# Hybrid decoder block on one core: plain pairs for differential attention and the first gates, GpSimd transfers in written order, normalising chunk by chunk, plain pairs emptied block by block

## The chip, the cores and the metric

One core of one Trainium2 chip runs the whole program. Its engines are PE (TensorE, matmul; PEld is its weight load), DVE (VectorE), ACT (ScalarE), POOL (GpSimd) and SP (SyncE), which here only issues transfers. The metric is the device time of one execution in microseconds, the median of three runs. A profile is one further execution, so sums are made against that execution's own time.

## What is computed

One decoder layer of width 2048 over 256 tokens, in float32:

```python
h = rmsnorm(x, norm_mix)
proj = h @ w_in                     # dq dk dv | conv in | rq rk rv rg | 3 x 2048 gates
ya = diff_attention(rope(dq), rope(dk), dv, lam)    # softmax(map 0) - lam * softmax(map 1)
yb = silu(layernorm(conv(ca * sigmoid(cb))))        # 31 taps, causal
yr = silu(rg) * groupnorm(retention(rope(rq), rope(rk), rv))
merged = sum(sigmoid(gates[i]) * (y @ w_branch[i])) # i = 0 ya, 1 yb, 2 yr
x = x + merged @ w_out
x = x + cross_attention(rmsnorm(x), rmsnorm(mem))   # wq, wkv, wo; 4 heads, 256 memory tokens
x = x + swiglu(rmsnorm(x))                          # w13: 2 x 5632 columns, w2
return rmsnorm(x, norm_final)
```

All weights are read from HBM once; the activations of the layer stay on the chip but for a few spills.

## The kernel before, in words

**One product.** A weight matrix is cut into column blocks of 512 and depth chunks of 512. A half chunk (256 deep, 128x1024 elements in the chip's layout) is loaded by SP into a tile `raw` (10 buffers), and is then split in two parts: ACT casts it to `wh` (high part, type fp32r) and DVE subtracts to get `wl` (the rest). The activations are held in the same two parts (`hi`, `lo` of an `Act`). A product is three matmuls of 128x512: high by high, high by rest, rest by high. A half chunk against both token halves is one *unit* of 12 matmuls. The parts are made up to LA = 4 units ahead of their matmuls.

**Plain and S pairs.** Column blocks go in pairs. In a plain pair (`win` with MODES0, function `block`) the two blocks run one after the other, each chunk costs 4 units, 48 matmuls for both blocks, and `evac` reads the PSUM tile `mm` (2 buffers) straight away. In an S pair (function `pair`) some chunks, marked S in MODES1 = "SNNN" and MODES2 = "SSNN", are done by a scheme with 7 products of block matrices in place of 8 (`quad_jobs`): 7 units of 6 matmuls, so 42. For these DVE adds raw tiles (2 per chunk), two GpSimd transfers add a quarter of the weights onto a raw tile (`f2`, line 367, whose sum is used by unit p7, and `f6`, line 383, whose sum is used by p4), 7 casts and 7 subtractions make the parts, four PSUM tiles `tp` take intermediate sums, and `join1`, `join5`, `join6`, `join7` (1 ACT copy and 5 DVE operations of 128x512) and two `done` (one DVE addition of 128x1024 each) put the result together before `evac` reads it from SBUF. The S chunks need factors of the activations (`factors`: 4 small DVE operations, a cast and a subtraction), kept in `shi` and `slo`.

**The first pair of a stage.** `pair_n` runs the first pair on activations that are not yet scaled by the row norm: for each of the four chunks first both halves of block 0, then both of block 1, and `after(c)` behind chunk c; `evac0` and `evac1` follow at the end. `normalise` meanwhile makes scaled copies (`xn` from `xa`; `x2n` from `x2T`) for the pairs that follow: at `after(1)` it waits for the norm, starts `spread` (which broadcasts it) and four tasks `chunk(c)`; each adds the parts, multiplies, splits again, and makes factors for the chunks in `sc`.

**Order of work.** All is emitted as a list of units and calls. Side work (rope, conv, attention, normalising) is written as Python generators; `pump` advances each by one step after every unit, `drain` and `need` run one to its end where its result is wanted. A list scheduler with a simulated clock then sets the order on each engine. SP's loads are held to the written order by `tc.keep_in_program_order` (`ld`); the DMAs that GpSimd issues are not.

**Stages.** In order: conv inputs (pair_n on blocks 8 and 6, then 9 and 7), retention of 2 groups (4 plain pairs), differential attention (`diff_qk(0)`, `win(4, 5, ...)`, `diff_qk(1)`, all MODES1), three times gates (2 S pairs, MODES2, each followed by two branch blocks), memory keys and values (4 S pairs on `w_kv`), `w_out` (2 S pairs), queries and cross attention, `w_o` (2 plain blocks and an S pair), SwiGLU (pair_n, then 10 S pairs on `w_13`, and between them twice 2 S pairs on `w_2` with `x2` reloaded by `load_x2`), and the last blocks of `w_2` with the final norm, for which `load_gf` and `load_x2` fetch six tiles.

Nearly every instruction is recorded under line 85, the wrapper that issues it, so groups are told apart by the tiles that they write and read. Line 93 is SP's load.

Of the kernel before, what the change touches and what calls it, by code (L numbers as in the profile page):

```python
# [44 lines left out]
class Act:  # L45


    def __init__(self):
        self.hi = None
        self.lo = None  # L50
        self.shi = None
        self.slo = None
        self.task = None


@with_exitstack
def trunk(ctx, tc, xT, xtok, memT, memtok, w_in, w_br, w_out, w_q, w_kv, w_o, w_13, w_2,
          prm, cst, decay, gfin, out):
    nc = tc.nc
# [29 lines left out]
    sc = Pinned(nc.scalar, "act" in PIN)  # L89
    ve = Pinned(nc.vector, "dve" in PIN)  # L90
    pe = Pinned(nc.tensor, "pe" in PIN)
    def ld(**kw):
        tc.keep_in_program_order(nc.sync.dma_start(**kw))

# [20 lines left out]
    active = []  # L115
    said = {}
    wants = {}
    cap = [4]

    def spawn(gen, want=1):  # L120
# [19 lines left out]
                step(g)  # L140

    def drain(g):
        if g in active:
            settle(cap[0] - wants[g], g)
            while step(g):
                pass
# [178 lines left out]
    def quad_jobs(pp, ps0, ps1, w0, w1, a):  # L325

        def unit(ps, key, k0, t, kind, fn, **w):
            def add():  # L330
                load(**w)
                u = add_unit([(ps, key, k0, t, kind)], a)
                u["alloc"] = alloc_tp1 if ps is pp else alloc_mm
                groups.append(([u], lambda: fn(u)))
                return u
            return add

        def alloc_tp1(ps, key):
            ps[key] = TP()

        b21, b22 = w0[:, 2:4, :], w1[:, 2:4, :]
        ix = {}

        def load(**k):
            for n, w in k.items():
                ix[n] = add_chunk(w)

        def add(o, x):
            ve.tensor_tensor(out=o, in0=o, in1=x, op=ALU.add)

        def parts(u, src):
            parts_of(u)
            hi_of(u, src)
            lo_of(u, src)

        t = {}

        def f1(u):
            t["a"] = raw(ix["b11"])
            parts(u, t["a"])  # L360
            raws.pop(ix["b11"])

        def f2(u):
            r = raw(ix["b21"])
            t["b"] = raw(ix["b12"])
            add(t["a"], t["b"])
            nc.gpsimd.dma_start(out=t["b"], in_=b22, accum_op=ALU.add)  # L367
            parts(u, r)
            raws.pop(ix["b21"])
            raws.pop(ix["b12"])  # L370

        def f5(u):
            parts(u, t["a"])

        def f3(u):
            r = raw(ix["b22"])
            add(t["a"], r)
            parts(u, r)
            raws.pop(ix["b22"])

        def f6(u):
            parts(u, t["a"])
            nc.gpsimd.dma_start(out=t["a"], in_=b21, accum_op=ALU.add)  # L383

        def f7(u):
            parts(u, t.pop("b"))

        def f4(u):
            parts(u, t.pop("a"))

        return dict(p1=unit(pp, 1, 0, 0, "n", f1, b11=w0[:, 0:2, :]),
                    p2=unit(ps0, 0, 2, 0, "n", f2, b21=b21, b12=w1[:, 0:2, :]), p5=unit(pp, 5, 0, 0, "s", f5),
                    p3=unit(ps1, 0, 0, 3, "s", f3, b22=b22), p6=unit(pp, 6, 0, 1, "s", f6),
                    p7=unit(pp, 7, 0, 2, "s", f7), p4=unit(ps0, 1, 2, 1, "n", f4))

# [78 lines left out]
    def pair_n(W0, W1, acts, evac0, evac1, after):  # L474

        ps0, ps1 = {}, {}
        us = []
        for c in range(len(acts)):
            us += half_jobs(ps0, [W0[c]], [acts[c]])
            us += half_jobs(ps1, [W1[c]], [acts[c]])  # L480
            call(lambda c=c: after(c))
        call(lambda: evac0(ps0["m"]))
        call(lambda: evac1(ps1["m"]))
        close(us)


    prm_t = cpool.tile([P, PCOLS], F32, name="prm_t")
# [29 lines left out]
    def load_actT(a, src, g, c):  # L517

        def gen():
            r = S4([P, 4, 256])  # L520
            nc.gpsimd.dma_start(out=r, in_=src[c])
            yield
            for k in range(0, 4, 2):
                actT_part(a, r, g, c, (k, k + 1))
                yield
        return gen()
# [99 lines left out]
        sc.copy(a.hi, q)  # L626
        ve.tensor_tensor(out=a.lo, in0=q, in1=a.hi.bitcast(F32), op=ALU.subtract)

    def normalise(src, dst, rs, sc=SC):

        st = {}
        freed = []

        def chunk(c):
            while len(freed) <= c:
                yield
            drain(st["task"])
            q = whole(src[c])
# [9 lines left out]

        def after(c):
            freed.append(c)  # L650
            if c == 1:
                rs()
                st["task"] = spawn(spread(st, rs.tile))
                for i in range(4):
                    dst[i].task = spawn(chunk(i))
        return after

    class Rstd:
# [202 lines left out]
    def win(n0, n1, modes, evac0, evac1):  # L861
# [3 lines left out]
        else:  # L865
# [1 line left out]
            block(w_in, n1, xn, evac1)  # L867

    pair_n([w_in[8, c] for c in range(4)], [w_in[6, c] for c in range(4)], xa, ev_cb(0, rsx), ev_ca(0, rsx),
           normalise(xa, xn, Rstd(rsx, lambda: drain(st_task)), (0,)))  # L870
    win(9, 7, MODES0, ev_cb(1), ev_ca(1))


# [32 lines left out]
    def ret_group(g):  # L906
        st = {}

        def ev_v(ps):
            st["v"] = act(ps, AF.Identity, None)  # L910
            d = S4([P, 4, 256])
            nc.gpsimd.dma_start(out=d, in_=decay[g])
            st["d"] = d

        def ev_g(ps):
# [59 lines left out]

    def ev_dv(g):
        def f(ps):
            dst2[g]["v"] = ps
            ya[g].task = spawn(diff_task(g, dst2[g]), 2)
        return f  # L980

    def diff_qk(g):
        win(0 + g, 2 + g, MODES1, ev_rope(dst2[g], "q", 32, 0), ev_rope(dst2[g], "k", 32, 0))

    def diff_task(g, st):
        drain(st["qt"])
# [76 lines left out]
    for g in range(2):  # L1063
        ret_group(g)
    diff_qk(0)
    win(4, 5, MODES1, ev_dv(0), lambda ps: dst2[1].update(v=ps))
    diff_qk(1)
    call(lambda: setattr(ya[1], "task", spawn(diff_task(1, dst2[1]), 2)))

# [37 lines left out]
            a.task = spawn(add_factors(a))  # L1107
        return f

    call(later(xn[1]))  # L1110
    for bi, (br, ys) in enumerate(((2, yr), (1, yb), (0, ya))):
        if bi == 1:
            call(split_yb)
        for nb in (0, 2):
            if bi == 2 and nb == 2:
                call(lambda: mtask.append(spawn(mem_stats())))
            win(18 + 4 * br + nb, 19 + 4 * br + nb, MODES2, ev_gate(nb), ev_gate(nb + 1))
            if bi == 2 and nb == 2:
                call(lambda: mem_chunks())
            for n in (nb, nb + 1):  # L1120
# [8 lines left out]
    mst = {}  # L1129

    def mem_stats():
        yield from tok_stats(memtok, rsm, nc.gpsimd.dma_start)
        yield from spread(mst, rsm)

    def mem_chunk(c):
        r = S4([P, 4, 256])
        nc.gpsimd.dma_start(out=r, in_=memT[c])
        drain(mtask[0])
        yield
        times(r, mst["rb"])  # L1140
# [11 lines left out]

    def ev_kv(dst):
        def f(x):
            nc.gpsimd.dma_start(out=dst, in_=x)
        return f

    def mT_factors():
# [13 lines left out]
    def residual(W, acts, xin, aT, gname, rs, parts, spill=None):  # L1172
# [3 lines left out]
        def ev(nb):  # L1176
            def f(ps):
# [2 lines left out]
                xs[nb] = r  # L1180
                if spill is not None:
                    xs[nb] = None
                    nc.gpsimd.dma_start(out=spill[nb], in_=r)

                def gen():
                    sumsq(r, parts[:, nb, :])
# [20 lines left out]
    def reload_x(nbs):  # L1207
        for nb in nbs:
            xre[nb] = S4([P, 2, 512])
            nc.gpsimd.dma_start(out=xre[nb], in_=xtok[nb])  # L1210

    x1T = [Act() for _ in range(4)]
    rs1 = cpool.tile([P, 2], F32, name="rs1")
# [25 lines left out]
    def prep_kv(h):  # L1239

        def gen():
            k, v = S4([P, 2, 512]), S4([P, 2, 512])
            nc.gpsimd.dma_start(out=k, in_=kM[h])
            nc.gpsimd.dma_start(out=v, in_=vM[h])
            yield
            yield from transposed(kT[h], blk(k), None)
            k = None
# [130 lines left out]
    def ev_w2(nb):  # L1378
        def f(ps):
            ve.tensor_tensor(out=ps, in0=ps, in1=x2[nb], op=ALU.add)  # L1380
            nc.gpsimd.dma_start(out=x2d[nb], in_=ps)
            x2[nb] = None
        return f

    def load_gf():
        for i in range(2):
            g = S4([P, 2, 512])
            nc.gpsimd.dma_start(out=g, in_=gfin[:, 2 * i:2 * i + 2, :])
            gf.append(g)
        gf.append(S4([P, 512]))  # L1390
        ve.memset(parts3, EPS)
# [12 lines left out]
    def load_x2(nbs):  # L1404
        for nb in nbs:
            x2[nb] = S4([P, 2, 512])
            nc.gpsimd.dma_start(out=x2[nb], in_=x2d[nb])

    def w2_group(lo):
        for nb in (0, 2):  # L1410
# [152 lines left out]
```

## Time and profile before

| | |
|---|---|
| median of 3 runs | 2087.9 us (2087.73 to 2093.46) |
| the profiled execution | 2088.45 us |
| its span (first to last instruction) | 2086.7 us |
| PE busy | 1999.3 us |
| DVE busy | 1727.0 us |
| ACT busy | 1146.6 us |
| POOL busy | 146.2 us |

Times in the trace count from the start of the span; 1.75 us of the execution lie outside it. In a row of the timeline the bracket says how long the engine stood idle before the instruction, and what ended that. PEclk is the clock granted to TensorE as a share of full speed.

### The profile page before, as it was taken

What the parts mean: (1) busy time and instruction counts of PE and PEld (TensorE: products, weight loads), DVE (VectorE), ACT (ScalarE), POOL (GpSimd) and SP (SyncE); (2) the same over time, 40 slices, a digit from 0 to 9 for tenths busy, and PEclk for the clock granted to TensorE, in tenths of its full rate; (3) what the DMA queues carried; (4) which work ended last, traced back from release to release, by engine and by line L of the source; (5) the groups of instructions that cost most, each with busy time, mean ns of one, the idle gap of its engine ahead of it and who ended that gap; (6) DMA issues with size and microseconds to landing.
All of it is one profiled execution on the core that took longest, in us unless ns stands there. A gap on an engine that the chain in (4) does not pass through costs nothing.

```text
span 2086.7 us, 25367 instructions
## 1 busy us (share of the span) xinstructions
PE 1999.3 (96%) x9039; PEld 1642.9 (79%) x9039; DVE 1727.0 (83%) x2101; ACT 1146.6 (55%) x1367; POOL 146.2 (7%) x186
## 2 busy tenths in 40 slices
PE   9799999888999999989989999998999999999988
PEld 6688887766778888778877888886888888888866
DVE  7896689987878878898969765889998999899854
ACT  6444354447655555655546554655665566555643
POOL 0000001000000000010101000000011101010100
PEclk9899999999999999999999999999999999999999
DMA  9465556564568777779889744766889888889871
GB/s 365 161 196 187 177 173 181 165 183 124 174 212 251 229 215 252 263 223 278 277 249 289 256 168 143 221 203 195 254 259 310 269 256 255 276 281 286 248 259 71
DMA packets 130303, 471.23 MB, mean 226 GB/s; under 512 B 14592, under 2 KB 14848, under 8 KB 130176
## 3 DMA queue, kind: packets, MB, share of 16 engines
q1 hardware_dynamic: 105552, 380.46, 51.6%
q0 software_dynamic: 24480, 89.14, 20.7%
q8 instruction: 71, 1.16, 0.2%
q14 instruction: 56, 0.46, 0.1%
q10 hardware_dynamic: 144, 0.01, 0.0%
HBM read 456.97 MB, written 12.58 MB: 225 GB/s over the span
## 4 chain that ended last, share of the span: by engine, by line
PE 55%; issue 15%; DVE 15%; DMA 9%; ACT 3%; POOL 2%; SPq 0%; POOLq 0%; ACTq 0%; DVEq 0%
PE mm L85 44%; PE tp L85 11%; DVE wl L85 7%; DVE s L85 6%; DMA raw<-in_w 5%; ACT wh L85 2%; DMA raw<-in_w_kv 2%; DVE raw L85 2%; DMA raw<-in_w_in 1%; ACT s L85 1%; POOL raw L367 1%; POOL raw L383 0%; ACT L85 0%; DMA raw<-in_w_out 0%; POOL tn L508 0%
## 5 line engine op out<-in xcount | busy, mean ns | idle before, releaser
L85 PE MATMUL mm<-wh,s 128*128 128x512 f32 x4428 | 1411.1, 393 | 49.6 <-ACT wh L85 27.4
L85 ACT CAST wh<-raw 128x1024 fp32r<-128x1024 f32 (+1 forms) x876 | 909.9, 1051 | 795.3 <-PE mm L85 495.3
L85 DVE TENSOR_TENSOR wl<-raw,wh 128x1024 fp32r<-128x1024 f32 (+1 forms) x876 | 1049.6, 1224 | 265.1 <-ACT wh L85 248.8
L85 PEld LDWEIGHTS mm<-wh,s 128*128 128x128 f32 x4428 | 837.3, 189 | 230.5 <-ACT wh L85 35.2
L85 PE MATMUL mm<-wl,s 128*128 128x512 f32 x2214 | 871.5, 394 | 22.2 <-DVE wl L85 22.1
L85 PEld LDWEIGHTS mm<-wl,s 128*128 128x128 f32 x2214 | 419.2, 189 | 116.5 <-DVE wl L85 30.3
L85 PE MATMUL tp<-wh,s 128*128 128x512 f32 x976 | 329.8, 396 | 0.0
L85 PEld LDWEIGHTS tp<-wh,s 128*128 128x128 f32 x976 | 185.3, 190 | 39.3 <-issue 0.7
L85 PE MATMUL tp<-wl,s 128*128 128x512 f32 x488 | 191.9, 393 | 0.0
L85 DVE TENSOR_TENSOR s<-s,s 128x1024 f32<-128x1024 f32 (+4 forms) x143 | 140.8, 993 | 8.6 <-ACT s L85 6.8
L85 DVE TENSOR_TENSOR raw<-raw,raw 128x1024 f32<-128x1024 f32 x114 | 139.0, 1225 | 9.0 <-DMA raw<-in_w_kv 5.4
L85 DVE TENSOR_TENSOR s<-tp,s 128x512 f32<-128x512 f32 (+1 forms) x182 | 121.1, 688 | 18.1 <-PE tp L85 10.7
L85 DVE TENSOR_TENSOR s<-mm,s 128x1024 f32<-128x1024 f32 (+1 forms) x79 | 94.6, 1197 | 20.5 <-PE mm L85 20.2
L85 DVE SCALAR_TENSOR_TENSOR s<-s,prm_t,s 128x256 fp32r<-128x256 f32 (+28 forms) x256 | 107.6, 477 | 0.0
L85 PEld LDWEIGHTS tp<-wl,s 128*128 128x128 f32 x488 | 92.9, 190 | 18.2
L85 ACT ACTIVATE s<-s 128x512 f32<-128x512 f32 (+1 forms) x62 | 48.2, 780 | 53.8 <-DVE s L85 43.0
L85 PE MATMUL tp<-cst_t,s 128*128 128x128 f32 x408 | 58.0, 277 | 3.2 <-ACT s L85 2.4
L85 PEld LDWEIGHTS tp<-cst_t,s 128*128 128x128 f32 x408 | 49.1, 142 | 13.1 <-ACT s L85 2.8
L85 PE MATMUL tp<-s,s 128*128 128x256 f32 (+4 forms) x348 | 55.8, 314 | 0.8 <-ACT s L85 0.8
L85 PEld LDWEIGHTS tp<-s,s 128*128 128x128 f32 (+1 forms) x348 | 47.5, 189 | 7.3 <-issue 1.6
L85 ACT COPY s<-tp 128x512 f32<-128x512 f32 (+1 forms) x73 | 38.0, 532 | 19.0 <-PE tp L85 17.4
L367 POOL DMA_DIRECT2D raw<-in_w x28 | 24.1, 862 | 311.5 <-DVE raw L85 208.8
(95 smaller groups left out, 545.9 us busy)
## 6 DMA issues: line engine op xcount, KB each, us to landing
raw<-in_w SPq DMA_DIRECT2D x264, 512.0 KB, 6.7
raw<-in_w_in SPq DMA_DIRECT2D x239, 512.0 KB, 4.7
raw<-in_w_kv SPq DMA_DIRECT2D x64, 512.0 KB, 6.2
raw<-in_w POOLq DMA_DIRECT2D x56, 512.0 KB, 8.2
raw<-in_w_br SPq DMA_DIRECT2D x48, 512.0 KB, 5.7
raw<-in_w_out SPq DMA_DIRECT2D x32, 512.0 KB, 7.1
raw<-in_w_q SPq DMA_DIRECT2D x32, 512.0 KB, 5.1
raw<-in_w_o SPq DMA_DIRECT2D x32, 512.0 KB, 3.9
```

The costliest lines, as they stand in the source:

```text
L85: i = f(*a, **k)
L367: nc.gpsimd.dma_start(out=t["b"], in_=b22, accum_op=ALU.add)
```

## The change

There are five edits.

1. The pairs of the differential attention and the first gate pair become plain (MODES0). The value block is then copied out of PSUM by ACT (`ev_dv`), and the second value block uses the same function.
2. `xn` gets no factors in `normalise` (its `sc` is empty). Both `xn[0]` and `xn[1]` get them by `later` ahead of the gates.
3. Every DMA that GpSimd issues goes through `gd`, which holds them to the order in which they are written.
4. `normalise` runs its chunks one behind the other (`gen`, `first`), and for the feed-forward part starts behind chunk 0 in place of chunk 1.
5. `pair_n` interleaves the two blocks for chunks 0 and 1 only; then it does chunks 2 and 3 of block 0 and empties block 0, then those of block 1, and empties it.

```diff
+    def gd(**kw):
+        tc.keep_in_program_order(nc.gpsimd.dma_start(**kw))
...
     def drain(g):
+        if g in first:
+            drain(first.pop(g))
         if g in active:
...
-            nc.gpsimd.dma_start(out=t["b"], in_=b22, accum_op=ALU.add)
+            gd(out=t["b"], in_=b22, accum_op=ALU.add)
...
-            nc.gpsimd.dma_start(out=t["a"], in_=b21, accum_op=ALU.add)
+            gd(out=t["a"], in_=b21, accum_op=ALU.add)
...
         ps0, ps1 = {}, {}
-        us = []
-        for c in range(len(acts)):
-            us += half_jobs(ps0, [W0[c]], [acts[c]])
-            us += half_jobs(ps1, [W1[c]], [acts[c]])
+        u0, u1 = [], []
+        for c in range(2):
+            u0 += half_jobs(ps0, [W0[c]], [acts[c]])
+            u1 += half_jobs(ps1, [W1[c]], [acts[c]])
             call(lambda c=c: after(c))
+        u0 += half_jobs(ps0, W0[2:], acts[2:])
         call(lambda: evac0(ps0["m"]))
+        for c in range(2, 4):
+            u1 += half_jobs(ps1, [W1[c]], [acts[c]])
+            call(lambda c=c: after(c))
         call(lambda: evac1(ps1["m"]))
-        close(us)
+        close(u0 + u1)
...
-    def normalise(src, dst, rs, sc=SC):
+    def normalise(src, dst, rs, sc=SC, at=0):
...
-            while len(freed) <= c:
+            while len(freed) <= c or c and dst[c - 1].gen in active:
                 yield
...
-            if c == 1:
+            if c == at:
                 rs()
                 st["task"] = spawn(spread(st, rs.tile))
                 for i in range(4):
-                    dst[i].task = spawn(chunk(i))
+                    dst[i].task = dst[i].gen = spawn(chunk(i))
+                    first[dst[i].gen] = dst[i - 1].gen if i else st["task"]
...
-           normalise(xa, xn, Rstd(rsx, lambda: drain(st_task)), (0,)))
+           normalise(xa, xn, Rstd(rsx, lambda: drain(st_task)), (), 1))
...
     def ev_dv(g):
         def f(ps):
-            dst2[g]["v"] = ps
-            ya[g].task = spawn(diff_task(g, dst2[g]), 2)
+            dst2[g]["v"] = act(ps, AF.Identity, None)
+            if g == 0:
+                ya[g].task = spawn(diff_task(g, dst2[g]), 2)
         return f
...
-        win(0 + g, 2 + g, MODES1, ev_rope(dst2[g], "q", 32, 0), ev_rope(dst2[g], "k", 32, 0))
+        win(0 + g, 2 + g, MODES0, ev_rope(dst2[g], "q", 32, 0), ev_rope(dst2[g], "k", 32, 0))
...
-    win(4, 5, MODES1, ev_dv(0), lambda ps: dst2[1].update(v=ps))
+    win(4, 5, MODES0, ev_dv(0), ev_dv(1))
...
-    call(later(xn[1]))
+    for c in SC:
+        call(later(xn[c]))
...
-            win(18 + 4 * br + nb, 19 + 4 * br + nb, MODES2, ev_gate(nb), ev_gate(nb + 1))
+            win(18 + 4 * br + nb, 19 + 4 * br + nb, MODES2 if bi or nb else MODES0, ev_gate(nb), ev_gate(nb + 1))
```

All other DMAs of GpSimd (decay tables, `memtok`, `memT`, stores and reloads of `kM` and `vM`, `xtok`, `x2d`, `gfin`) are put through `gd` in the same way.

## Rows read from the trace of the kernel before

**Rows 1.** The page, part 1: busy time of each engine.
```profile
PE 1999.3 (96%) x9039; PEld 1642.9 (79%) x9039; DVE 1727.0 (83%) x2101; ACT 1146.6 (55%) x1367; POOL 146.2 (7%) x186
```

**Rows 2.** Busy time by stretch: start:end, length, engines' busy (instructions), clock, DMA.
```profile
330.00:560.00 230.00, 206.42 (x923) 163.27 (x922) 203.02 (x364) 126.88 (x191) 17.17 (x13) 0.94 0.56 165
66.00:300.00 234.00, 234.00 (x1073) 194.57 (x1073) 184.15 (x313) 100.97 (x109) 3.12 (x3) 0.99 0.55 176
630.00:660.00 30.00, 30.00 (x134) 24.86 (x133) 24.25 (x23) 17.80 (x19) 1.73 (x3) 1.00 0.85 247
1375.00:1440.00 65.00, 54.79 (x239) 45.00 (x238) 55.22 (x60) 34.50 (x37) 3.50 (x4) 0.92 0.51 145
26.00:76.00 50.00, 37.97 (x163) 30.98 (x162) 36.48 (x45) 25.98 (x37) 1.42 (x2) 0.86 0.71 266
```

**Rows 3.** Timeline of PE: start, length, what, count, idle before and its releaser.
```profile
65.66 0.79 PE L85 MATMUL mm<-wh,s 128*128 128x512 f32 x1 [12.03 <-ACT s L85]
...
1051.88 0.79 PE L85 MATMUL mm<-wh,s 128*128 128x512 f32 x1 [5.81 <-ACT wh L85]
...
1420.44 0.80 PE L85 MATMUL mm<-wh,s 128*128 128x512 f32 x1 [10.21 <-ACT s L85]
...
1999.88 0.80 PE L85 MATMUL mm<-wh,s 128*128 128x512 f32 x1 [9.14 <-ACT wh L85]
```

**Rows 4.** Busy time in half-clock stretches; the sum row covers five between 366.8 and 500.
```profile
56.20:69.90 13.70, 4.24 (x10) 3.37 (x11) 10.30 (x12) 5.68 (x6) 0.71 (x1) 0.50 0.35 122
1049.50:1056.30 6.80, 4.42 (x10) 3.46 (x11) 3.54 (x4) 3.65 (x4) 0.00 (x0) 0.50 0.76 219
1414.70:1425.00 10.30, 4.56 (x11) 3.60 (x12) 7.31 (x8) 5.13 (x6) 0.00 (x0) 0.50 0.32 107
1995.00:2005.20 10.20, 5.17 (x11) 3.84 (x12) 5.34 (x5) 5.88 (x6) 0.00 (x0) 0.50 0.47 139
...
sum 27.60, PE 22.79 PEld 17.66 DVE 26.70 ACT 9.50 POOL 1.86; mean PE 4.56 PEld 3.53 DVE 5.34 ACT 1.90 POOL 0.37
```

**Rows 5.** Timeline of ACT around the ends of the two `pair_n`.
```profile
61.99 1.04 ACT L85 CAST s<-s 128x1024 fp32r<-128x1024 f32 x1 [3.69 <-DVE s L85]
...
64.34 1.26 ACT L85 ACTIVATE s<-mm,rsx 128x512 f32<-128x512 f32 x2
...
1419.12 1.27 ACT L85 ACTIVATE s<-mm,rs 128x512 f32<-128x512 f32 x2
```

**Rows 6.** Groups of instructions by shape: count, busy us, mean ns, idle before.
```profile
L85 DVE TENSOR_TENSOR wl<-raw,wh 128x1024 fp32r<-128x1024 f32 x874 | 1048.2, 1225 | 262.7 <-ACT wh L85 246.4 <-DMA raw<-in_w_in 6.6 <-DMA raw<-in_w_q 4.5
L85 ACT CAST wh<-raw 128x1024 fp32r<-128x1024 f32 x874 | 908.6, 1052 | 793.0 <-PE mm L85 495.3 <-DMA raw<-in_w 60.5 <-DMA raw<-in_w_in 55.1
L85 DVE TENSOR_TENSOR raw<-raw,raw 128x1024 f32<-128x1024 f32 x114 | 139.0, 1225 | 9.0 <-DMA raw<-in_w_kv 5.4 <-DMA raw<-in_w_out 3.3
L85 DVE TENSOR_TENSOR s<-mm,s 128x1024 f32<-128x1024 f32 x75 | 91.8, 1225 | 5.2 <-PE mm L85 5.0
L85 DVE TENSOR_TENSOR s<-tp,s 128x512 f32<-128x512 f32 x124 | 82.8, 688 | 13.8 <-PE tp L85 10.7 <-DMA x2d<-s 3.1
```

**Rows 7.** Timeline of POOL and of ACT at the last S pair.
```profile
1972.40 0.86 POOL L383 DMA_DIRECT2D raw<-in_w  x1 [13.86 <-DVE wl L85]
1972.94 1.42 POOL L1388 DMA_DIRECT2D s<-in_gfin  x2
1974.02 2.43 POOL L1407 DMA_DIRECT2D s<-x2d  x4
1976.41 0.95 POOL L383 DMA_DIRECT2D raw<-in_w  x1
...
1998.78 4.83 ACT L85 CAST wh<-raw 128x1024 fp32r<-128x1024 f32 x5 [16.24 <-DMA raw<-in_w]
```

**Rows 8.** Timeline of POOL and of ACT at the end of the memory pairs.
```profile
1038.91 0.53 POOL L1210 DMA_DIRECT2D s<-in_xtok  x1 [12.23 <-issue]
1039.44 1.83 POOL L383 DMA_DIRECT2D raw<-in_w_kv  x2
...
1050.78 1.99 ACT L85 CAST wh<-raw 128x1024 fp32r<-128x1024 f32 x2 [10.19 <-DMA raw<-in_w_kv]
```

**Rows 9.** The page, part 6: DMA issues, KB each, median us to landing.
```profile
raw<-in_w POOLq DMA_DIRECT2D x56, 512.0 KB, 8.2
```

More of the change, by code (lines that the diff above doesn't have):

```diff
@@ L53, in __init__ @@
         self.task = None
+        self.gen = None
 @with_exitstack
@@ L117, in trunk @@
     wants = {}
+    first = {}
     cap = [4]
@@ L520, in gen @@
             r = S4([P, 4, 256])
-            nc.gpsimd.dma_start(out=r, in_=src[c])
+            gd(out=r, in_=src[c])
             yield
@@ L911, in ev_v @@
             d = S4([P, 4, 256])
-            nc.gpsimd.dma_start(out=d, in_=decay[g])
+            gd(out=d, in_=decay[g])
             st["d"] = d
@@ L1131, in mem_stats @@
     def mem_stats():
-        yield from tok_stats(memtok, rsm, nc.gpsimd.dma_start)
+        yield from tok_stats(memtok, rsm, gd)
         yield from spread(mst, rsm)
@@ L1136, in mem_chunk @@
         r = S4([P, 4, 256])
-        nc.gpsimd.dma_start(out=r, in_=memT[c])
+        gd(out=r, in_=memT[c])
         drain(mtask[0])
@@ L1154, in f @@
         def f(x):
-            nc.gpsimd.dma_start(out=dst, in_=x)
+            gd(out=dst, in_=x)
         return f
@@ L1182, in f @@
                     xs[nb] = None
-                    nc.gpsimd.dma_start(out=spill[nb], in_=r)
+                    gd(out=spill[nb], in_=r)
                 def gen():
@@ L1209, in reload_x @@
             xre[nb] = S4([P, 2, 512])
-            nc.gpsimd.dma_start(out=xre[nb], in_=xtok[nb])
+            gd(out=xre[nb], in_=xtok[nb])
     x1T = [Act() for _ in range(4)]
@@ L1242, in gen @@
             k, v = S4([P, 2, 512]), S4([P, 2, 512])
-            nc.gpsimd.dma_start(out=k, in_=kM[h])
-            nc.gpsimd.dma_start(out=v, in_=vM[h])
+            gd(out=k, in_=kM[h])
+            gd(out=v, in_=vM[h])
             yield
@@ L1380, in f @@
             ve.tensor_tensor(out=ps, in0=ps, in1=x2[nb], op=ALU.add)
-            nc.gpsimd.dma_start(out=x2d[nb], in_=ps)
+            gd(out=x2d[nb], in_=ps)
             x2[nb] = None
@@ L1387, in load_gf @@
             g = S4([P, 2, 512])
-            nc.gpsimd.dma_start(out=g, in_=gfin[:, 2 * i:2 * i + 2, :])
+            gd(out=g, in_=gfin[:, 2 * i:2 * i + 2, :])
             gf.append(g)
@@ L1406, in load_x2 @@
             x2[nb] = S4([P, 2, 512])
-            nc.gpsimd.dma_start(out=x2[nb], in_=x2d[nb])
+            gd(out=x2[nb], in_=x2d[nb])
     def w2_group(lo):
```

## The prediction

> **What bounds the kernel now.** I read the page first. PE is busy 96% of the span, DVE 83% [rows 1], so a gain must come out of PE's idle time or out of fewer matmuls. The pace of a full PE is read from a stretch in which it never waits: 134 matmuls in 30 us, 0.224 us each [rows 2]. Next I went through PE's timeline for waits, because 4% of idle time can be many small gaps or a few large ones. It is a few large ones: 12.03 us at the end of the first `pair_n`, 5.81 at the end of the memory pairs, 10.21 at the end of the second `pair_n`, 9.14 behind the last S pair [rows 3], and a region from 330 to 560, the differential attention and the first gate pair, where PE is busy 206.42 of 230 us [rows 2]. Last I read the granted clock. Around each large gap it is at 0.50, that is 1.2 in place of 2.4 GHz, and PE's busy time inside such a stretch does half its work: 4.24, 4.42, 4.56 and 5.17 us at the four gaps, 22.79 us in five stretches inside the region [rows 4]. So a gap costs its idle time and about half of the slow busy time behind it: 14.1, 8.0, 12.5 and 11.7 us for the four, and 23.6 + 11.4 = 35.0 us for the region.
>
> **Plain pairs for differential attention and the first gates.** This adds matmuls. A chunk done plainly has 48 instead of 42; three pairs give up one S chunk, the gate pair two, so 5 x 6 = 30 matmuls, 6.7 us at the full pace, all on the path.
>
> What it takes from DVE is much more. An S chunk has 7 subtractions and 2 additions of raw tiles against 4 subtractions: 5 operations of 1.2 us [rows 6], 6.0 us, five times: 30. Each of the four pairs loses five joins of 0.67 us and two `done` of 1.22 us [rows 6], 5.8 us, four times: 23. Together 53 us; one addition of 1.2 us comes back for the factors of `xn[0]`, and its factor work, some 4 us, moves here out of the first stage. ACT loses 15 casts of 1.04 us [rows 6] and four copies, and gains two PSUM copies of the value blocks, which I price like a cast: 2 us, hidden, as ACT is busy 127 of 230 us [rows 2]. If that cover were gone they would cost those 2 us. The ten GpSimd additions of weights go too. The evacuations now read PSUM and not SBUF; I count that at nothing, since two `mm` buffers leave an evacuation a whole block of 96 matmuls (21 us) to finish.
>
> Is DVE what PE waits for here? It is busy 203.02 of 230 us [rows 2], 88%, and by list scheduling it is busiest just where units are short (6 matmuls for one subtraction). About 48 of the removed 53 us net of the moved factors lie in this region or just ahead of it. That leaves 155 us of DVE in a region of 230 - 35.0 + 6.7 = 202 us, 77%. The stretch from 66 to 300, plain pairs with conv and retention beside them, has DVE at 184.15 of 234, 79%, and PE is never idle in it [rows 2]. That is the nearest row, and by it all 35 us go. From the other side, the chains of exponentials and table loads in the attention tasks stay, and their waits cannot be told apart from DVE's load in advance; if only a third of the waits went, 12 us would. I take 80%, nearer to the plain stretch: 28 - 6.7 = **21 us gained** (bounds 5 and 28).
>
> **Block by block, and chunk by chunk.** At the end of the first `pair_n` PE waits for ACT, which waits for DVE: the evacuation at 64.34 stands in ACT's queue behind the cast of a later chunk, which waited 3.69 us for DVE [rows 5]. Both `mm` buffers are full until then, so the next block cannot start. After the change block 0 ends 48 matmuls (11 us) earlier and is emptied while block 1 runs, so the next block has a buffer at once. What is late next is then `xn` or the weights' parts, both DVE's. DVE is busy 36.48 us of 26 to 76 [rows 2], less some 3 us for the factors that leave; the stretch without the stall would be 50 - 14.1 = 35.9 us long. It fits, with little to spare. I take **11 us** (bounds 4 and 14).
>
> The second `pair_n` has the same picture: ACT evacuates at 1419.12 [rows 5], and PE starts 1.3 us later [rows 3]. But here the factors stay, and an S pair with its dense DVE work follows at once. From 1375 to 1440 DVE is busy 55.22 of 65 us [rows 2], so even a DVE that never pauses gives back at most 9.8 of the 12.5 us. Starting at chunk 0 brings work forward by 48 matmuls, 11 us, into time in which DVE has room. I take **6 us** (bounds 0 and 9.8).
>
> **Written order on GpSimd's queue.** At the last S pair the second addition of line 383 is issued at 1976.41, behind six loads of 512 KB for the final stage [rows 7]. They are written later than it, as their calls stand behind the pair, and the scheduler drew them forward. ACT's next cast waits 16.24 us for it [rows 7], and PE 9.14. The median from issue to landing on this queue is 8.2 us [rows 9]; landing would be near 1984.6 and the cast some 14 us earlier than 1998.78, which is more than PE's whole wait. The final loads then land later, but their first user is dozens of matmuls away. I take **11 us** of 11.7 (bounds 9 and 12).
>
> The Trainium skill prices such a transfer otherwise: DMA: Bandwidth & Descriptors, Anatomy of one DMA, fits 2.0 us plus the bytes at 436 GB/s for a GpSimd transfer, which for 512 KB would be an estimated 3.2 us, with the addition landing near 1979.6. The trace's 8.2 us [rows 9] does not agree, and decides. By either figure the cast comes before PE has run out, so the term of the sum would be the same.
>
> At the end of the memory pairs a reload of `xtok` stood 12.23 us on POOL, and both additions of line 383 are issued straight behind it, at 1039.44 [rows 8]. ACT waits 10.19 us for them, PE 5.81. In written order those reloads come behind the additions. But the reloads' bytes move into the next pair, and the first addition may not have been ready much sooner than 1039: I take **6 us** of 8.0 (bounds 0 and 8).
>
> What is put behind something now: stores and reloads of `kM`, `vM`, `x2d` and `xtok` were issued where they were ready and are now in line with the additions of lines 367 and 383. A store written between the two additions of line 367 waits for the last `done` of the pair before, and holds the second one up by some microseconds. This touches about nine pairs. Their sums are wanted only by unit p7, the fifteenth of the pair, and parts are made 4 units ahead, so I charge **2 us** in all; from below nothing, from above the price of one late addition as at 1046, 5.8 + 2.2 = 8.0 us, at each of nine pairs, 72 us.
>
> **The sum.** 21 + 11 + 6 + 11 + 6 - 2 = 53 us off the profiled execution's 2088.45 us, 2035 us. The median of the runs is 0.5 us below that execution, which changes nothing.
>
> **The rivals.** *DVE takes over.* The waits are not for a PSUM buffer or an order but for DVE, and come back one step later. For: DVE above 85% from 330 to 560 and from 1375 to 1440 [rows 2]. Against: the plain stretch without a wait. It gives 6 us at the first `pair_n`, 5 in the region, 0 at the second, 3 at the memory pairs, 11 at the end, less 2: 23 us, 2065 us.
>
> *Everything goes.* All five waits vanish with their slow clock: 14.1 + 28.3 + 8.0 + 9.8 + 11.7 = 72 us, 2016 us, and a few of the small waits of the second gate pair may go with them: 2012.
>
> *The queue blocks.* In written order one load that must wait for its buffer holds up every addition behind it. The 12.23 us that a reload stood on the queue [rows 8] show that such waits occur. If nine pairs pay 8.0 us each, the 55 us of the other terms turn into a loss of 17: 2105 us. It decides from about seven pairs on. Against it: stalls of that kind appear in the trace where a later transfer was drawn forward, not where the order was the written one. The Trainium skill speaks for it (PSUM — Partial Sum Buffer, Engine vs sequencer instructions: the queues of ScalarE, VectorE and GpSimd are strictly first in, first out), and the two additions that left right behind the waiting reload agree [rows 8].
>
> **How the numbers follow.** The forecast, 2020 to 2050, has 0.66; everything goes 0.08; DVE takes over, 2050 to 2075, 0.20; the queue blocks 0.06, most of it slower than before. What a measurement of this kernel tells from no change is about 0.3%, 6 us. Faster by more than that: 0.91; within it 0.04; slower 0.05. The range that leaves out some 2 in 10 is 2013 to 2063.
>
> **What would show it.** In the changed profile PE's waits of 12.03, 10.21 and 9.14 us should be gone or below 3 us, with the clock at 1.00 there; line 383's second addition should stand ahead of the `gfin` loads; the region of the differential attention should hold 30 more matmuls and PE waits below 8 us, with DVE near 77%. POOL's waits ahead of line 367 should not make ACT wait on `raw` more than before. The prediction is wrong if the waits stand again under DVE `wl`, or if ACT waits on DMA in the `w_2` and memory pairs.

## The result, and the profile after

The changed kernel takes 2030.3 us at the median (2027.9 to 2031.2, four runs) against 2087.8 for the kernel before: ratio 0.972, 95% interval 0.970 to 0.974. The forecast was 2035 us, in a range of 2013 to 2063. The kernel gained 5 us more than the sum had it, but single terms are off by 10 us and more, in both directions; the experiments below are about those.

The profiled execution of the changed kernel took 2031.2 us with a span of 2029.5. First its page, part 1, which answers to [rows 1]:

```profile
PE 1990.1 (98%) x9069; PEld 1641.5 (81%) x9069; DVE 1680.8 (83%) x2049; ACT 1122.2 (55%) x1344; POOL 133.1 (7%) x176
```

PE has 30 matmuls more, as counted, and DVE is busy 46 us less. PE's share rose to 98%. Next the busy time by stretch (start:end, length, each engine's busy time and instructions, clock, DMA). The two rows cover the differential attention with the first gate pair, and the second gate pair; they answer to the first row of [rows 2]:

```profile
322.50:521.00 198.50, 198.50 (x974) 162.58 (x973) 161.83 (x310) 110.46 (x177) 5.84 (x5) 1.00 0.52 166
521.00:598.00 77.00, 72.27 (x313) 58.81 (x312) 61.11 (x74) 42.60 (x53) 5.06 (x5) 0.96 0.70 207
```

In the first stretch PE never waits, with DVE at 82%. Last, the timeline of PE: the wait at the first `pair_n`, two at the second gate pair and two behind the second `pair_n`, which answer to [rows 3]:

```profile
57.51 0.79 PE L86 MATMUL mm<-wh,s 128*128 128x512 f32 x1 [4.66 <-ACT s L86]
...
545.23 0.50 PE L86 MATMUL mm<-wl,s 128*128 128x512 f32 x1 [0.99 <-DVE wl L86]
555.25 0.80 PE L86 MATMUL mm<-wh,s 128*128 128x512 f32 x1 [3.59 <-ACT wh L86]
...
1389.83 0.50 PE L86 MATMUL mm<-wh,s 128*128 128x512 f32 x1 [1.76 <-ACT wh L86]
1411.87 0.76 PE L86 MATMUL mm<-wh,s 128*128 128x512 f32 x1 [7.02 <-DVE s L86]
```

The waits of 5.81 and 9.14 us are gone. Of the 12.03 us at the first `pair_n`, 4.66 are left. The 10.21 us at the second are gone from their place, but a wait of 7.02 us stands one pair later.

To see where the time went I compare, in each trace, the start of the same 128x512 matmul. The columns are times in the trace of before, and the numbers say how much earlier (minus) or later that matmul starts, in us. They come from one profiled execution each; those of e1_plain (2050.2 us) and e1_pairn (2087.3 us) were the longest of their runs, 8.5 and 5.8 us above the median, so these two rows are on the low side. The last three rows are the experiments of the next section.

```
before at    90    325    640    930   1100   1390   1425   1590   1980   2083
after      -7.6   -7.5  -42.0  -39.1  -48.2  -49.2  -60.8  -49.5  -45.0  -57.2
e1_order   +0.9   +0.9   +7.8   +7.2   -0.2   -1.0   -1.0   -0.3   +2.4   -9.8
e1_plain   -0.8   -0.7  -42.4  -38.8  -40.4  -40.9  -41.1  -41.2  -40.0  -38.3
e1_pairn   -7.8   -7.7   -5.2   -2.2   -1.1   -1.5  -13.1   -4.4   -2.5   -1.2
```

In the row of after: 7.5 us gained at the first `pair_n`; 34.5 from 325 to 640, of which 31.5 are the differential attention with the first gate pair and 3.0 the second gate pair; 3 lost in the memory pairs; 9 to 10 gained at the `xtok` reloads; 11.6 gained at the second `pair_n` and 11.3 given back right behind it; 4.4 lost in the `w_2` pairs; 12.2 gained at the last S pair.

### The profile page after: what moved, and what is told of

It is laid out like the page before. It is cut to its first block, busy times and chain, and to the rows that moved or that the text cites. A ratio compares the mean times of both kernels' runs of the same rounds, so it can differ in the third digit from the quotient of the medians.

```text
span 2029.5 us, 25287 instructions
## 1 busy us (share of the span) xinstructions
PE 1990.1 (98%) x9069; PEld 1641.5 (81%) x9069; DVE 1680.8 (83%) x2049; ACT 1122.2 (55%) x1344; POOL 133.1 (7%) x176
## 4 chain that ended last, share of the span: by engine, by line
PE 50%; issue 9%; DVE 6%; DMA 5%; POOL 1%; ACT 1%; ACTq 0%; POOLq 0%; DVEq 0%
PE mm L86 38%; PE tp L86 12%; DMA raw<-in_w 4%; DVE wl L86 3%; DVE s L86 3%; DMA raw<-in_w_out 1%; DVE raw L86 1%; ACT wh L86 1%; POOL raw L94 1%; DMA s<-in_memtok 0%; DMA raw<-in_w_in 0%; ACT s L86 0%; ACTq L1572 0%; POOL s L94 0%; POOL x2d L94 0%
## 5 line engine op out<-in xcount | busy, mean ns | idle before, releaser
L86 PE MATMUL mm<-wh,s 128*128 128x512 f32 x4528 | 1440.1, 393 | 22.5 <-ACT wh L86 8.7
L86 ACT CAST wh<-raw 128x1024 fp32r<-128x1024 f32 (+1 forms) x861 | 893.6, 1051 | 754.3 <-PE mm L86 462.7
L86 DVE TENSOR_TENSOR wl<-raw,wh 128x1024 fp32r<-128x1024 f32 (+1 forms) x861 | 1030.1, 1220 | 265.2 <-ACT wh L86 252.0
L86 PEld LDWEIGHTS mm<-wh,s 128*128 128x128 f32 x4528 | 854.5, 189 | 204.8 <-ACT wh L86 13.5
L86 PE MATMUL mm<-wl,s 128*128 128x512 f32 x2264 | 889.5, 393 | 7.6 <-DVE wl L86 7.4
L86 PE MATMUL tp<-wh,s 128*128 128x512 f32 x896 | 298.5, 392 | 0.0
L86 PEld LDWEIGHTS tp<-wh,s 128*128 128x128 f32 x896 | 168.2, 188 | 34.7 <-issue 0.3
L86 PE MATMUL tp<-wl,s 128*128 128x512 f32 x448 | 174.5, 389 | 0.0
L86 DVE SCALAR_TENSOR_TENSOR s<-s,prm_t,s 128x256 fp32r<-128x256 f32 (+24 forms) x256 | 105.5, 469 | 0.0
L94 POOL DMA_DIRECT2D raw<-in_w x56 | 49.4, 882 | 439.4 <-DVE wl L86 187.9
```

What stands on the lines that cost most here:

```text
L86: i = f(*a, **k)
L94: tc.keep_in_program_order(nc.gpsimd.dma_start(**kw))
```

## The experiments

### One part of the change at a time

Theory 1: the parts act separately, and each is worth what the shifts show. Three kernels are the kernel before with one part of the diff each.

**The written order alone.** Every `nc.gpsimd.dma_start(...)` of the kernel before becomes `gd(...)`, as in the diff.

> The kernel before with the written order on GpSimd's queue alone. Theory 1 (the gains of the parts are separate, so each is worth here what the shifts between the two traces show): end 12.2 us gained, xtok reloads 10.1 us gained, w_2 pairs 4.4 us lost, memory pairs between 0 and 3.5 us lost; together 14 to 18 us off 2087.8, so 2070 to 2074 us. By the prediction's own terms it would be 11 + 6 - 2 = 15 us, 2073. Rival (the written order pays only because the other edits took DVE's load away, and blocks the queue by itself): 2082 us or more, with waits of ACT for raw in the w_2 and memory pairs of over 10 us.

Measured: 2078.7 us against 2087.5, ratio 0.994 (0.992 to 0.997). That is 9 us and not 14 to 18. The rival falls: ACT's longest wait for `raw` in the memory and `w_2` pairs is 4.3 us. The `xtok` reloads gave 7.4 us and the end 12.2, close to what was expected. But 6.9 us were lost from 325 to 640, where I had expected nothing. The timeline of PE there:

```profile
592.12 0.93 PE L85 MATMUL tp<-cst_t,s 128*128 128x128 f32 x2 [2.81 <-DVE s L85]
600.41 0.51 PE L85 MATMUL mm<-wh,s 128*128 128x512 f32 x1 [2.55 <-ACT wh L85]
```

And the timeline of POOL just ahead of it:

```profile
590.08 1.66 POOL L511 TENSOR_TENSOR tn<-tn,nhalf 128x8 f32<-128x8 f32 x1 [37.46 <-DVE tn L85]
591.71 1.81 POOL L93 DMA_DIRECT2D raw<-in_w_in  x2
```

Both additions of line 383 leave straight behind an instruction that is no transfer: the power that makes the reciprocal root for the group norm of the differential attention. GpSimd stood idle for 37.46 us ahead of it, until VectorE had its operand `tn` ready. `keep_in_program_order` pins a transfer behind the instruction written before it on the same engine, whatever that is. In the kernel before, the two additions of this pair leave at 573.5 and 581.2, ahead of the power at 587.2:

```profile
573.51 0.86 POOL L383 DMA_DIRECT2D raw<-in_w_in  x1 [22.28 <-DVE wl L85]
581.19 0.86 POOL L383 DMA_DIRECT2D raw<-in_w_in  x1 [6.82 <-DVE wl L85]
587.16 1.66 POOL L508 TENSOR_TENSOR tn<-tn,nhalf 128x8 f32<-128x8 f32 x1 [5.11 <-DVE tn L85]
```

So the written order has a price at the second gate pair. The same is seen in the changed kernel, for one of the two additions:

```profile
528.88 0.86 POOL L94 DMA_DIRECT2D raw<-in_w_in  x1 [14.54 <-DVE wl L86]
545.35 1.66 POOL L519 TENSOR_TENSOR tn<-tn,nhalf 128x8 f32<-128x8 f32 x1 [15.61 <-DVE tn L86]
546.97 0.89 POOL L94 DMA_DIRECT2D raw<-in_w_in  x1
```

The Trainium skill (PSUM — Partial Sum Buffer, Engine vs sequencer instructions) calls this queue strictly first in, first out, and the rows agree: the addition leaves as soon as the power ends. ACT's cast stands 12.89 us for that addition:

```profile
554.15 1.99 ACT L86 CAST wh<-raw 128x1024 fp32r<-128x1024 f32 x2 [12.89 <-DMA raw<-in_w_in]
```

**The plain pairs alone.** The edits of the diff to `diff_qk`, `ev_dv`, the gates' modes, `later` and the factors of `xn`.

> The kernel before with the plain pairs for differential attention and the first gate pair alone (the factors of both xn chunks made at the gates). Theory 1 (separate gains): 31.5 us in the region and 3.0 at the second gate pair, 34.5 us off 2087.8, so 2053 us (2050 to 2057), with no wait of PE in the differential attention. The prediction's step: 21 us, 2067 (not below 2060). Rival (the part of the gain above 28 us came from the written order or from the earlier start of xn): 2060 to 2067 us, with waits of PE left in the region.

Measured: 2041.7 us (2038.7 to 2050.2), ratio 0.976 (0.973 to 0.979): 46 us by the medians, more than any of the numbers. In the profiled execution 41.7 us lie between 325 and 640. Its two stretches, cut as those of after above:

```profile
324.30:527.70 203.40, 203.40 (x995) 166.64 (x994) 166.66 (x321) 112.47 (x178) 5.87 (x5) 1.00 0.52 163
527.70:597.60 69.90, 69.30 (x313) 56.92 (x313) 60.89 (x74) 43.11 (x53) 7.16 (x5) 1.00 0.76 229
```

PE waits for nothing in the first stretch, as in after. In the second it needs 69.9 us for the same 313 instructions for which the changed kernel needs 77.0. Plain pairs without the written order are worth 41.7 us here, with it 34.5; the written order by itself costs 6.9. So the numbers of theory 1 were wrong for both kernels, but the parts do add up, with another account than I had: the plain pairs gain 42 us, and the written order takes 7 of them back.

**The two edits to `pair_n` and `normalise` alone.**

> The kernel before with normalising chunk by chunk and pair_n emptied block by block alone. Theory 1 (the first place gains 6.8 us, the second gains 12.6 us and gives 12.2 back one pair later because DVE has no room there): about 7 us off 2087.8, so 2081 us (2079 to 2083), with a wait of PE of 5 to 9 us at the end of the first S pair of the feed-forward. Rival (the give-back came from the written order of the transfers, and is absent here): 19 us, 2068 us, without that wait. The prediction's step: 11 + 6 = 17 us, 2071.

Measured: 2081.6 us, ratio 0.997 (0.995 to 0.999), 6 us. The first place gains 7.8 us. The second gains 11.6 and gives 8.8 back at the end of the next S pair, on the same wait as in after:

```profile
1458.40 0.77 PE L86 MATMUL mm<-wh,s 128*128 128x512 f32 x1 [7.01 <-DVE s L86]
```

That is what theory 1 expected. The written order is not what gave the gain back; the rival falls.

### The price of GpSimd's arithmetic

Theory 2: the 7 us are the power's. This kernel keeps the written order among transfers alone (`NOSYNC` stands for an edge that orders the issue and waits for nothing):

```diff
+    prev = [None]
...
     def gd(**kw):
-        tc.keep_in_program_order(nc.gpsimd.dma_start(**kw))
+        i = nc.gpsimd.dma_start(**kw).ins
+        if prev[0] is not None:
+            tc.add_manual_dep(i, prev[0], NOSYNC, reason="written order of the DMAs")
+        prev[0] = i.name
```

The changed kernel ran beside it once more, as a mark:

> The changed kernel once more, as the mark for the three kernels beside it: 2030 us (2027 to 2033).

It took 2029.9 us (2028.8 to 2035.2), ratio 0.971 (0.969 to 0.973).

> The changed kernel with the transfers on GpSimd's queue kept in written order among themselves alone, and no longer behind GpSimd's arithmetic; the one instruction that moves is the power for the group norm of the differential attention, from ahead of the second addition of line 383 in the second gate pair to behind it. Theory 2 (the written order cost 7 us there, since that addition had to wait for the power, and the power for VectorE): the waits of 0.99 and 3.59 us at 545 and 555 and the slow clock behind them go, 7 us off, 2023 us (2021 to 2026). Rival (the attention task's load on VectorE makes those waits, whatever the order): 2030 us, the same waits.

Measured: 2023.9 us, ratio 0.968 (0.966 to 0.970), 6 us below the mark. By the shift of the matmuls, 7.2 us go at the second gate pair, and in this execution, the shortest of the four, another 3.5 in the memory pairs. Timeline of POOL:

```profile
528.93 0.86 POOL L96 DMA_DIRECT2D raw<-in_w_in  x1 [14.83 <-DVE wl L86]
533.22 0.85 POOL L96 DMA_DIRECT2D raw<-in_w_in  x1 [3.42 <-DVE wl L86]
545.12 3.70 POOL L525 TENSOR_TENSOR tn<-tn,nhalf 128x8 f32<-128x8 f32 x1 [11.05 <-DVE tn L86]
```

The second addition leaves at 533.22 and not at 546.97, and PE's waits of 0.99 and 3.59 us are gone; the longest there is 0.53. On POOL this one instruction changed its place, and all other engines keep their order until 544 us, so the cause is shown.

### What is left at the first `pair_n`

The rows of ACT in the changed kernel, which answer to the first two of [rows 5]:

```profile
50.17 1.06 ACT L86 CAST wh<-raw 128x1024 fp32r<-128x1024 f32 x1 [1.62 <-PE mm L86]
52.89 1.04 ACT L86 CAST wh<-raw 128x1024 fp32r<-128x1024 f32 x1 [1.66 <-PE mm L86]
53.84 1.04 ACT L86 CAST s<-s 128x1024 fp32r<-128x1024 f32 x1
54.90 1.28 ACT L86 ACT_TABLE_LOAD   x1
56.19 1.26 ACT L86 ACTIVATE s<-mm,rsx 128x512 f32<-128x512 f32 x2
```

Block 0 is complete at about 41.5, but the sigmoid that empties it runs at 56.19. On ACT it stands behind five casts of weights that are written after it, and these wait for the buffers that PE frees. Theory 3: the scheduler's order is what keeps the buffer full. The kernel adds, for ScalarE, an edge from the evacuation to everything written later:

```diff
+                if self.eng is nc.scalar and behind:
+                    tc.add_manual_dep(i.ins, behind[0], NOSYNC, reason="behind")
+                if self.eng is nc.scalar:
+                    last[0] = i.ins.name
...
-        call(lambda: evac0(ps0["m"]))
+        call(lambda: (evac0(ps0["m"]), behind.append(last[0])))
...
-        call(lambda: evac1(ps1["m"]))
+        call(lambda: (evac1(ps1["m"]), behind.clear()))
```

It stands in `pair_n`, so it acts on both of them.

> The changed kernel with every ScalarE instruction that is written behind the first pair_n's sigmoid kept behind it, until the pair_n's end. Theory 3 (the first pair_n kept a wait of 4.66 us because the scheduler put the sigmoid behind five casts of weights written after it): the sigmoid runs some 6 us earlier, the wait and the slow clock behind it go, 7 us off, 2023 us (2021 to 2027). Rival (the cast of the second xn chunk, which is written ahead of the sigmoid, waits for VectorE, and now holds up the weights too): the wait stays or grows, 2030 us or more.

Measured: 2019.2 us, ratio 0.965 (0.964 to 0.967), 11 us below the mark and below the range I gave. Timeline of ACT at the first `pair_n`:

```profile
49.83 1.05 ACT L88 CAST s<-s 128x1024 fp32r<-128x1024 f32 x1 [4.24 <-DVE s L88]
50.89 1.28 ACT L88 ACT_TABLE_LOAD   x1
52.19 1.26 ACT L88 ACTIVATE s<-mm,rsx 128x512 f32<-128x512 f32 x2
53.34 4.84 ACT L88 CAST wh<-raw 128x1024 fp32r<-128x1024 f32 x5
```

and of PE, its one wait there:

```profile
54.44 0.50 PE L88 MATMUL mm<-wh,s 128*128 128x512 f32 x1 [1.22 <-ACT wh L88]
```

The sigmoid runs 4 us earlier, PE's wait falls from 4.66 to 1.22 us, and 5.3 us are gained there. The rival had something too: the cast ahead of the sigmoid waits 4.24 us for VectorE, and the weights wait behind it. Theory 3 holds for most of what was left. Another 5 us lie behind the second `pair_n`, where the order is kept too and I had not looked for a gain.

### Who gave the gain back behind the second `pair_n`

Theory 4: VectorE has no room there. The kernel does the next pair plainly (`ev_a` then writes the silu to a new tile, as its input stands in PSUM):

```diff
+            elif i == 1:
+                block(w_13, i, x2n, ev_a(i))
+                block(w_13, 11 + i, x2n, ev_b(i))
```

> The changed kernel with the first S pair of the feed-forward as two plain blocks: 12 more matmuls, 2.7 us, and some 18 us less work for VectorE behind the second pair_n. Theory 4 (the gain at the second pair_n was given back because VectorE, with the factors and the dense S pair, has no room there): the waits of 1.76 and 7.02 us and the slow clock of 10.2 us behind them go, 1.8 + 7.0 + 5.1 - 2.7 = 11 us off, 2019 us (2017 to 2023). Rival (the wait moves on with the factors to the next S pair): 2030 to 2033 us, with a wait of 5 us or more one pair later.

Measured: 2023.6 us, ratio 0.968 (0.966 to 0.970), 6 us below the mark and less than the 11 expected. The wait of 7.02 us is gone and none comes one pair later, so the rival falls. By the shift of the matmuls 3.5 us are lost again in the `w_2` pairs. Busy time from 1330 to 1412 in after:

```profile
1330.00:1412.00 82.00, 73.22 (x327) 60.08 (x325) 76.65 (x81) 47.05 (x49) 5.21 (x6) 0.97 0.71 203
```

in this kernel:

```profile
1330.00:1412.00 82.00, 82.00 (x371) 67.94 (x370) 66.66 (x69) 44.96 (x49) 1.80 (x2) 1.00 0.60 189
```

and in the kernel of the section before, with ScalarE's order kept, which runs 7.7 us ahead here, from the same matmul on:

```profile
1322.30:1404.30 82.00, 79.43 (x349) 64.21 (x348) 76.59 (x81) 49.62 (x51) 5.22 (x6) 1.00 0.66 192
```

With 10 us less on DVE, PE never waits. But in the third row DVE is as busy as in the first (76.59 and 76.65 us), and PE has 6 us more. So "no room" is too simple: the order matters as well. The plain pair also has no `done` and no late addition, so this kernel alone does not show that the load is the cause. A row of ACT and three of DVE in after show an order that hurts:

```profile
1388.73 3.91 ACT L86 CAST wh<-raw 128x1024 fp32r<-128x1024 f32 x4 [6.14 <-DMA raw<-in_w]
...
1389.81 2.36 DVE L86 TENSOR_TENSOR wl<-raw,wh 128x1024 fp32r<-128x1024 f32 x2 [3.37 <-ACT wh L86]
...
1399.03 2.35 DVE L86 TENSOR_TENSOR raw<-raw,raw 128x1024 f32<-128x1024 f32 x2
...
1410.51 2.35 DVE L86 TENSOR_TENSOR s<-mm,s 128x1024 f32<-128x1024 f32 x2
```

DVE stands still for 3.37 us, for a cast that waits for a late second addition; then additions and parts of the next pair come ahead of the two `done` at 1410.51, on which the PSUM buffer depends. Theory 5: it is that order alone. The kernel keeps everything that is written for VectorE behind a `done` of this one pair behind it, to the end of the next pair, with the same edge as above:

```diff
+                if self.eng is nc.vector:
+                    if behind:
+                        tc.add_manual_dep(i.ins, behind[0], NOSYNC, reason="behind")
+                    last[0] = i.ins.name
...
                 ve.tensor_tensor(out=x, in0=ps["m"], in1=x, op=ALU.add)
+                if hold[0]:
+                    behind[:] = [last[0]]
```

> The changed kernel with nothing on VectorE that is written behind a `done` of the first S pair of the feed-forward put ahead of that `done`; the first of the two moves eight instructions forward. Theory 5 (VectorE had room behind the second pair_n, but the scheduler put the next pair's additions and parts ahead of the `done`, on which the PSUM buffer and PE wait): the wait of 7.02 us and the slow clock behind it go, 9 us off, 2021 us (2018 to 2024). Rival (theory 4, VectorE has no room there): what was pushed behind is late instead, and waits of the same sum stand under the weights' parts, 2028 to 2032 us.

Measured: 2029.8 us, ratio 0.971 (0.969 to 0.972): no gain. The first `done` runs at 1401.05, PE's wait of 7.02 us falls to 1.12, and 9 us are gained at that place; but 6 of them are lost again one pair later, on the same kind of wait, and the rest is within the noise of the medians:

```profile
1410.09 0.50 PE L89 MATMUL mm<-wh,s 128*128 128x512 f32 x1 [1.12 <-ACT wh L89]
...
1452.25 0.77 PE L89 MATMUL mm<-wh,s 128*128 128x512 f32 x1 [3.23 <-DVE s L89]
```

Theory 5 falls as it was put, and with it a plain "order" explanation. What the three kernels suggest together: VectorE comes out of the second `pair_n` with a backlog; the plain pair, which takes work away from it, ends the wait for good, and to reorder at the end of the pair moves most of it on by one pair. That the backlog is the cause is not shown. That the kernel with ScalarE's order does better with the same load on DVE is measured (the pause of 3.37 us on DVE is 1.76 there), but why it keeps its gain stays open.

**Where the normalising starts.** The second `normalise` begins after chunk 1, as the first one does: `normalise(x2T, x2n, Rstd(...), SC, 1)`.

> The changed kernel with the normalising behind the second pair_n begun after its chunk 1, as the first pair_n has it, and not after chunk 0. The prediction's step (the start at chunk 0 brings the work forward by 48 matmuls, 11 us, into time in which VectorE has room): PE waits for x2n at the pair_n's end, and 4 to 10 us are lost, 2034 to 2040 us. Rival (emptying block by block alone makes the gain at the second pair_n): 2027 to 2033 us, without a wait of over 2 us at the pair_n's end.

Measured: 2033.8 us (2032.1 to 2036.0), ratio 0.973 (0.971 to 0.975). By the medians 4 us are lost (3 by the ratios), by the shift of the matmuls in the profiled execution 1.6; the interval overlaps the mark's. PE waits at the end of the `pair_n`:

```profile
1370.00 0.80 PE L86 MATMUL tp<-wh,s 128*128 128x512 f32 x1 [3.21 <-ACT s L86]
1376.22 0.76 PE L86 MATMUL mm<-wh,s 128*128 128x512 f32 x1 [2.10 <-ACT s L86]
```

The matmuls lie 12.9 us late at that place, and 12 of these come back at the next pair, whose wait of 7.02 us is gone. So the start at chunk 0 does make the gain at the second `pair_n`, as the prediction said, and block by block alone does not. It looks like the same backlog again, paid at the end of the `pair_n` or one pair later.

### The small losses in the `w_2` pairs

The stores and reloads of `x2d` between these pairs go back to the scheduler's order (`nc.gpsimd.dma_start` in `ev_w2`, and in `load_x2` as the `w_2` pairs call it).

> The changed kernel with the stores and reloads of x2d between the w_2 pairs left to the scheduler, as before the change; the reloads for the final stage stay in written order. Theory (the written order cost the 4.4 us that the two w_2 stages lost): 4 us off, 2026 us, without the waits of 1.04, 0.50, 0.40 and 0.66 us there. Rival (these small waits come with any new order of the other engines; the kernel with the new pair_n alone lost 2.8 us there without the written order): 2029 to 2031 us.

Measured: 2028.5 us, ratio 0.970 (0.969 to 0.972), not told apart from the mark. From 1470 to 1950 the matmuls of its trace keep their distance to those of after (-3.2 and -3.1 us); a wait of 2.52 us takes the place of the small ones. The written order there costs nothing, and the loss of 4.4 us is not explained.

### Two edits together

> The changed kernel with two edits of the earlier kernels together: the transfers in written order among themselves alone, and ScalarE's instructions not put ahead of the first evacuation in either pair_n. Theory (the two gains are separate, 7 us at the second gate pair, 5 us at the first pair_n and 6 us at the second): 2030 - 7 - 11 = 2012 us (2009 to 2016), with no wait of PE over 2 us in the whole span. Rival (the order behind the second pair_n comes out otherwise again): a wait of 5 us or more there, 2018 to 2022 us.

Measured: 2014.2 us (2010.3 to 2015.2), ratio 0.963 (0.961 to 0.965), against 0.971 (0.969 to 0.973) of the mark. The forecast of 2012 is inside its runs, and it beats both kernels. Against after, its matmuls gain 3.6 us at the first `pair_n`, 7.2 at the second gate pair, 2 in the memory pairs and some 5 behind the second `pair_n`. A wait of 2.23 us in the memory pairs and one of 2.09 behind the second `pair_n` are left, so "no wait over 2 us" is missed by a little. PE's waits behind the second `pair_n`:

```profile
1363.78 0.50 PE L88 MATMUL tp<-wl,s 128*128 128x512 f32 x1 [1.31 <-DVE wl L88]
1378.67 0.50 PE L88 MATMUL mm<-wh,s 128*128 128x512 f32 x1 [1.44 <-ACT wh L88]
1395.84 0.47 PE L88 MATMUL mm<-wh,s 128*128 128x512 f32 x1 [2.09 <-DVE s L88]
```

## Why the prediction was right or wrong

**Plain pairs: 21 us said, 31.5 measured in the region it named, and 41.7 with the second gate pair and without the written order.** The 30 matmuls are right, and the mechanism fits: of the 23.6 us of waits in before's region 14.8 ended with DVE's `wl`, and all went. (The plain pairs take the late additions and the `done` away together with DVE's load; no run tells these apart.) The step that failed is "I take 80%, nearer to the plain stretch": all of the waits went. The nearest row, the stretch of plain pairs with DVE at 79% and no wait [rows 2], was the answer, and the bound it gave, 28, was still 3.5 us short; the rows of before account for 35.0 us, and 31.5 + 6.7 = 38.2 came. The other 3 us were pauses too short to be a row: outside the slow stretches a 128x512 matmul of before's region starts every 0.236 us, in after's every 0.232, and a 128x128 every 0.110 and 0.097. The second fault is the cut at 560: the waits of the second gate pair went too, though it stayed an S pair, and I named them only in a rival. DVE fell by less than I counted, from 203.0 to 161.8 us, and stands at 82% and not 77. The count was right (25 + 20 + 8 - 1 = 52 instructions fewer), the price per instruction was not: back to back, two subtractions take 2.36 us and four take 4.63, some 1.14 each and not 1.2, which is most of the gap between the 52 us counted and the 46 that went. Two readings were slightly off and change no term: a join is 0.69 us [rows 6], not 0.67, and DVE's 55.22 of 65 us from 1375 to 1440 [rows 2] is 85%, not above it.

**First `pair_n`: 11 said, 6.7 to 7.8 measured.** "The next block has a buffer at once" was the step that failed. Writing the evacuation earlier doesn't place it earlier on ACT: the scheduler drew five casts of weights ahead of it. With their order kept, 5.3 us more came.

**Second `pair_n`: 6 said, 0.3 kept.** The start at chunk 0 works as said. What I called the dense DVE work that "follows at once" was the right worry, but I set it against the gain at the place itself, as a limit of 9.8 us. The whole 11.6 us came, and 11.3 were paid back one pair later. That is in kind the rival "DVE takes over", at one place of five; how much of it is DVE's load and how much its order stays open.

**The end: 11 said, 12.2 measured.** The second addition leaves ahead of the final loads, as the timeline of POOL shows; PE doesn't wait there. It answers to [rows 7]:

```profile
1931.53 0.86 POOL L94 DMA_DIRECT2D raw<-in_w  x1 [3.14 <-DVE wl L86]
1932.07 1.43 POOL L94 DMA_DIRECT2D s<-in_gfin  x2
1933.15 2.43 POOL L94 DMA_DIRECT2D s<-x2d  x4
```

**Memory pairs and `xtok`: 6 said; 9 to 10 in after, above the bound of 8.0, and 7.4 with the written order alone.** The mechanism is the one of [rows 8]: the reloads no longer wait on the queue for their buffers, but leave behind the additions. POOL in after:

```profile
993.51 0.85 POOL L94 DMA_DIRECT2D raw<-in_w_kv  x1 [7.63 <-DMA raw<-in_w_kv]
997.67 0.85 POOL L94 DMA_DIRECT2D raw<-in_w_kv  x1 [3.32 <-DVE wl L86]
...
1023.85 1.07 POOL L94 DMA_DIRECT2D s<-in_xtok  x2
```

**New queue waits: 2 said, 7 at a single place.** I went through the transfers on GpSimd's queue and left out its arithmetic. The rival "the queue blocks" is right in kind, at one pair, with a price near the 8.0 us I gave for one late addition; what blocked was not a load or a store. The price I did put down, for the stores in the `w_2` pairs, was not to be found when the order of these transfers was set free.

That the sum was close is in part luck, since faults of opposite sign met: +21 at the plain pairs (with the second gate pair), +3 at `xtok` and +1 at the end, against -4, -6 and -5 at the two `pair_n` and on the queue, and 7 us lost in the `w_2` and memory pairs that no term of mine had.

## What to carry over

An order pinned on a queue counts for every instruction of that engine: before pinning transfers, list its arithmetic too and ask what that waits for. A wait that ends behind a busy engine has to be followed to the end of the next stage, since a gain at one place can be paid back there, as 11.3 of 11.6 us were here. And an evacuation written earlier is only earlier if nothing written later is drawn ahead of it; the order of the instructions on its engine has to be read.

## What was not expected of the hardware

The same pattern of short waits can cost TensorE's clock in one execution and not in another. In the first memory pair, before and after show nearly the same waits (0.94, 1.50, 0.46, 2.23 and 0.96, 1.50, 0.46, 2.08 us). Busy time of the matching stretches, before:

```profile
894.00:903.00 9.00, 6.70 (x31) 4.96 (x29) 9.00 (x12) 3.27 (x4) 0.00 (x0) 1.00 1.00 268
903.00:911.00 8.00, 5.17 (x23) 3.76 (x23) 8.00 (x10) 5.15 (x9) 0.86 (x1) 1.00 0.48 103
```

and after:

```profile
851.60:860.60 9.00, 6.54 (x31) 4.85 (x29) 9.00 (x11) 3.25 (x5) 0.00 (x0) 1.00 0.98 263
860.60:868.60 8.00, 5.45 (x12) 3.67 (x13) 8.00 (x9) 4.78 (x7) 0.85 (x1) 0.56 0.52 109
```

The first stretch holds 31 matmuls in both. In the second the clock stays at 1.00 (2.4 GHz) before and falls to 0.50 (1.2 GHz) after, 0.56 as the mean of the stretch, with 23 matmuls in 8 us against 12. In after the half clock lasts 10.2 us, in a second execution of the same kernel 6.8. The kernel with the written order alone has the waits of after (0.96, 1.52, 0.46 and 2.08 us), and its clock stays at 1.00 there: it loses nothing in these pairs. So the half clock is the 3 us that the memory pairs lost. What decides it is not shown by any run here.
